# Two more blocks in an SBUF arena, router weights loaded later, and the sync queue in written order behind the router

## The chip, the cores and the metric

The kernel runs on one core of a Trainium2 chip. The metric is the device time of one execution in microseconds. The kernel before took 1211.18 us (median of three runs, 1209.35 to 1215.85).

## The reference

One layer of a streaming encoder for 256 tokens of width 1024: two token mixers with one input projection, a merge by sigmoid gates, a layer norm, then a mixture of 32 experts of which each token takes four, and a second layer norm. Cut to what matters:

```python
mod = silu(c) @ w_ada + b_ada                       # shift1, scale1, gate1, shift2, scale2, gate2
h = x * (1 + scale1) + shift1
q_a, k_a, v_a, c_q, c_kv, k_rope, g_a, g_b = split(h @ w_in)
y_a = chunked_relpos_attention(q_a, k_a, v_a, rel_bias)
y_b = mla_attention(c_q, c_kv, k_rope, positions, ...)
merged = sigmoid(g_a) * (y_a @ w_branch_a) + sigmoid(g_b) * (y_b @ w_branch_b)
x = layer_norm(ALPHA * x + gate1 * (merged @ w_out), ln1_g, ln1_b)
h = x * (1 + scale2) + shift2
logits = h @ w_router + b_router                    # top 4 of 32, softmax over the four
g = min(xb @ w_gate[e] + b_gate[e], 7); up = clip(xb @ w_up[e] + b_up[e], -7, 7)
y = ((up + 1) * g * sigmoid(1.702 * g)) @ w_down[e] + b_down[e]
x = layer_norm(ALPHA * x + gate2 * weighted_sum(y), ln2_g, ln2_b)
```

Each expert has three float32 matrices of 1024 by 1024, so the experts alone are 403 MB of weights.

## The kernel before

**The arena.** Large buffers are blocks of 128 partitions by 2048 float32 values, 1 MB each. There are NB = 20 of them. `al()` hands out the block that has been free longest, `fr()` gives one back. The list PLACES says in which order 18 of them lie in SBUF; the other two (STAY) lie apart. Whatever is loaded, split or computed up to the router lives in such blocks. A load into a block waits until the last reader of its former content is done.

**The stages.** Modulation and the first projection come first (`modulate`, `project`), then attention, gates and the second part of the modulation (`attend`, `z_pair`, `ada2`), whose instructions a scheduler puts in order when the program is built. Then come the merge and the router, written out by hand inside a manual schedule of TensorE, ScalarE, VectorE, GpSimd and SyncE (SP). There `load_branch` and `load_wo` fetch projection weights, `mod_rows` writes the modulation rows to DRAM (tensor `rowd`) and reads them back as columns and as the broadcast rows gate1 and gate2, `o_part` is the output projection, and `route`, `count` and `place` choose the experts. `mod_cols` multiplies the router weights `wr` by the modulation.

**The first two experts** (30 and 31, group "s") are fixed: `load_fixed` fetches their 24 blocks (gate, up and down, four quarters each for two experts) while merge and router still run. In the page and in the matmul names, `sg`, `su` and `sd` are their gate, up and down products. Each product has steps k = 0 to 7, and after each odd step two blocks are given back.

**The other 30 experts** are sorted by how many tokens chose them and run in 13 groups, e0 to e12, of two or three experts. `sort_b` writes the sorted list to `order_i`. For each group SP reads the experts' numbers from it into registers (`nc.sync.value_load`, L1442), and uses them in the addresses of the weight loads (`load_group`, L1126). These loads go to pairs of neighbouring blocks, tensors `wt0` to `wt8`, 2 MB each. Pair d lies over the places 2d and 2d + 1 of PLACES, and `al2()` takes the pair that has been free longest. So each product of a group of two experts takes four pairs.

In the second stretch, from the fixed experts to the last group, only TensorE is under the manual schedule (`pe_cm`, L1383). SP's instructions there stand where the scheduler put them. All DMAs but two are issued by SP, which runs its queue in order: a load that waits holds back all that stands behind it. ScalarE issues the two others, ln1_g and ln1_b at L1080 and L1081, 512 KB each.

Of the kernel before, what the change touches and what calls it, by code (L numbers as in the profile page):

```python
# [8 lines left out]
F32 = mybir.dt.float32  # L9
# [8 lines left out]
P = 128  # L18
D = 1024
S = 256  # L20
E = 32
# [8 lines left out]
SCALE_A = 64.0 ** -0.5  # L30
SCALE_B = 96.0 ** -0.5
CAP = 64
NB = 20
BLK = 2048

STAY = (NB - 2, NB - 1)
PLACES = [10, 8, 1, 2, 0, 12, 13, 16, 11, 7, 4, 14, 5, 15, 6, 9, 17, 3]
FREQS = [
    1.0, 0.5623413324356079, 0.3162277638912201, 0.17782793939113617,
    0.10000000149011612, 0.05623413249850273, 0.03162277489900589, 0.017782794311642647,  # L40
# [28 lines left out]
def bcast_rows(ap, n=P):  # L69
    return bass.AP(tensor=ap.tensor, offset=ap.offset, ap=[[0, n]] + [list(a) for a in ap.ap])  # L70
# [3 lines left out]
def tile_layer(  # L74
# [30 lines left out]
    nc = tc.nc  # L105
    V, A, G, T, SP = nc.vector, nc.scalar, nc.gpsimd, nc.tensor, nc.sync

    const = ctx.enter_context(tc.tile_pool(name="const", bufs=1, side="left"))
# [10 lines left out]
    def ps_t(tag, bufs, name):  # L119
# [7 lines left out]
    first = {i: (aw if i in STAY else ar).tile([P, BLK], F32, tag=f"blk{i}", bufs=1, name=f"blk{i}_0")  # L127
             for i in STAY + tuple(PLACES)}
    freed = {i: i - NB for i in range(NB)}
    clock = [0]  # L130
# [15 lines left out]
    def fr(*blocks):  # L146
        for i in blocks:
            clock[0] += 1
            assert i not in freed
            freed[i] = clock[0]  # L150
# [4 lines left out]
    def ps_b(name):  # L155
        return ps_t("B", nb[0], name)
# [33 lines left out]
    def load_start(b):  # L190
        av, wv = [], []
        for i in range(2):
            v, r = al()
            v = v.rearrange("p (k m) -> p k m", k=8)
            SP.dma_start(v, wada_v[:, :, i * D + b * 256:i * D + (b + 1) * 256])
            av.append((v, r))
        for kk in range(2):
            v, r = al()
            SP.dma_start(v[:, 0:NZ], win_v[:, 2 * b + kk, 1024:1024 + NZ])
            wv.append((v, r))  # L200
        return av, wv
# [13 lines left out]
    LS = [load_start(0), load_start(1)]  # L215
    rows2 = p2.tile([16, P], F32, name="rows2")
    c2 = const.tile([P, 6, 2, 8], F32, name="c2")
    wr = const.tile([P, 8, E], F32, name="wr")
    br_b = const.tile([P, E], F32, name="br_b")
    pos_i = p2.tile([P, 2], I32, name="pos_i")  # L220
    with nc.allow_non_contiguous_dma("one position per partition"):
# [53 lines left out]
    for j in range(4):  # L275
        ps = ps_b(f"xT{j}")
        for kk in range(2):
            for t in range(2):
                k = 2 * j + kk
# [18 lines left out]
    def modulate(b):  # L298
        av, wv = LS[b]
        pm = ps_b(f"gemv{b}")  # L300
        for s in range(2):
            for i in range(2):
                for j in range(4):
                    k = 2 * j + i
                    T.matmul(pm[32 * j:32 * j + 32, s * 256:(s + 1) * 256], crep[:, k, :], av[s][0][:, k, :],
                             start=(i == 0), stop=(i == 1))
        fr(av[0][1], av[1][1])
        md = p2.tile([P, 512], F32, tag="md", bufs=2, name=f"md{b}")
        V.tensor_copy(md, pm)
        pt = ps_b(f"gemvT{b}")  # L310
        for i in range(4):
            T.matmul(pt[:, i:i + 1], md[:, i * P:(i + 1) * P], pick, start=True, stop=True)
        V.tensor_add(sh1v[:, :, 2 * b:2 * b + 2], pt[:, 0:4].rearrange("p (s k) -> p s k", s=2),
                     badv[:, :, 2 * b:2 * b + 2])
        for kk in range(2):
            k = 2 * b + kk
            h32 = p2.tile([P, S], F32, tag="h32", bufs=3, name=f"h32_{k}")
            V.tensor_scalar(h32, xT[:, k, :], sh1[:, 8 + k:9 + k], sh1[:, k:k + 1], op0=ALU.mult, op1=ALU.add)
            split(h32, hTh[:, k, :], hTl[:, k, :], "V")
# [22 lines left out]
    def load_biases():  # L342
        v, r = al()
        for i, b in enumerate((b_gate, b_up, b_down)):
            SP.dma_start(v[32 * i:32 * i + 32, 0:D], b[0])
        return v, r
# [14 lines left out]
    for b in range(4):  # L361
        if b + 2 < 4:
            LS.append(load_start(b + 2))
        if b == 0:
            bias_raw = load_biases()
        if b == 1:
            SP.dma_start(rows2[0:8, :], ln1_g.rearrange("o (k p) -> (o k) p", p=P))
            SP.dma_start(rows2[8:16, :], ln1_b.rearrange("o (k p) -> (o k) p", p=P))
            SP.dma_start(wr, w_router[0].rearrange("(k p) e -> p k e", p=P))
            with nc.allow_non_contiguous_dma("eight values per partition"):  # L370
                SP.dma_start(c2[:, 0, 1, :], ln1_g[0].rearrange("(p k) -> p k", k=8))
                SP.dma_start(c2[:, 1, 1, :], ln1_b[0].rearrange("(p k) -> p k", k=8))
            SP.dma_start(br_b, bcast_rows(b_router[0]))
        if b + 1 < 4:
            modulate(b + 1)
        project(b)
        if b == 1:
            split_biases(*bias_raw)
# [351 lines left out]
    p3 = p3_cm.__enter__()  # L730
# [12 lines left out]
    def mod_rows():  # L743
        for st in range(2):
            ps = ps_b(f"mod2_{st}")
            for j in range(4):
                T.matmul(ps[32 * j:32 * j + 32, :], ones[:, 0:32], acc_b[st][0][:, j * 512:(j + 1) * 512],
                         start=True, stop=True)
            V.tensor_add(rows32[:, st, :], ps, badd[:, st, :])
        fr(acc_b[0][1], acc_b[1][1])  # L750
        fr(ms_r)
        rowd = dram.tile([4 * D], F32, name="rowd")
        for st in range(2):
            SP.dma_start(rowd[st * 2 * D:(st + 1) * 2 * D].rearrange("(j n) -> j n", j=4), rows32[0:P:32, st, :])
        with nc.allow_non_contiguous_dma("a column from a row"):
            SP.dma_start(c2[:, 2:4, 1, :], rowd[D:3 * D].rearrange("(i p k) -> p i k", i=2, k=8))
            for i in range(2):
                SP.dma_start(c2[:, 2 + i, 0, :], rowd[(1 + i) * D:(2 + i) * D].rearrange("(k p) -> p k", p=P))
        SP.dma_start(gate1, bcast_rows(rowd[0:D]))
        SP.dma_start(gate2, bcast_rows(rowd[3 * D:4 * D]))  # L760

    wrs = p3.tile([P, 8, 2, E], F32, name="wrs")
    wrsum = p3.tile([P, 2 * E], F32, name="wrsum")
    gsum = p3.tile([P, E], F32, name="gsum")
# [21 lines left out]
    engines = {e.engine for e in (T, A, V, G, SP)}  # L786
# [12 lines left out]
    def load_fixed(n):  # L799

        for _ in range(n):
            kind, kq, j = fixed_todo.pop(0)
            v, r = al(stay=kind == 0)
            v = v.rearrange("p (k n) -> p k n", k=2)
            SP.dma_start(v, rows_of(weights[kind], E - 2 + j)[:, 2 * kq:2 * kq + 2, :])
            fixed[kind][0][j].append(v)
            fixed[kind][1][j].append(r)
# [2 lines left out]
    load_branch(2)  # L810
    load_branch(3)
    load_fixed(3)
    mod_rows()
    split_branch(1)
    split_branch(2)
# [283 lines left out]
    def open_pairs():  # L1099

        assert all(i in freed for i in PLACES)
        for d in range(len(PLACES) // 2):
            pairs[d] = max(freed[i] for i in PLACES[2 * d:2 * d + 2])
        ar_cm.__exit__(None, None, None)
# [275 lines left out]
        if i < len(GROUPS):  # L1380
            tokens[i] = gather(f"e{i}", group_slots(i))

    pe_cm = tc.manual_schedule(engines={T.engine})  # L1383
    pe_cm.__enter__()
    expert_group("s", segments((64, 64)), gather("s", None), lambda t, j: wtok[:, t, E - 2 + j:E - 1 + j], fixed_w,
                w_bias(sel0.rearrange("p a n -> p (a n)")), {("g", 0): sort_a, ("g", 3): sort_b, ("g", 7): sort_c},
# [134 lines left out]
```

## Time and profile before

| what | value |
|---|---|
| median of three runs | 1211.18 us |
| the profiled execution | 1212.23 us |
| its span, first to last instruction | 1210.5 us |
| mean granted TensorE clock | 0.935 |
| TensorE busy | 1049.7 us, 87% |
| VectorE busy | 372.6 us, 31% |
| HBM read | 462.24 MB, 383 GB/s over the span |

Busy shares are means over stages that have different limits. The page's second part cuts the span into 40 slices of 30.3 us: the DMA engines move 426 GB/s in nearly every slice from the eleventh on, and between 197 and 416 GB/s in the third to tenth. So the first quarter of the time and the rest are read separately.

### The profile page before, as it was taken

Reading aid. Unit: us, or ns where it says so; the run is one execution under the profiler, and the core shown is the slowest. Engines: PE = TensorE matmul, PEld = TensorE weight load, DVE = VectorE, ACT = ScalarE, POOL = GpSimd, SP = SyncE. Lnnn points to the kernel's source line nnn. Section 1 sums busy time; section 2 is a strip of 40 time slices with the busy share of each in tenths; the row PEclk is TensorE's granted clock in tenths of the full one; section 3 lists DMA queues with packets and bytes.
Section 4 is the critical chain, followed back from the end, with each engine's and each line's share of the span. In section 5 each row is a group of like instructions: output and inputs, shape, how many; then the busy total and the mean of one; then the engine's idle time right before and its main releaser. Section 6 shows DMA issues by size and latency. Waiting matters only on the chain.

```text
span 1210.5 us, 18672 instructions
## 1 busy us (share of the span) xinstructions
PE 1049.7 (87%) x7991; PEld 475.7 (39%) x7991; DVE 372.6 (31%) x751; ACT 176.3 (15%) x363; POOL 96.8 (8%) x120
## 2 busy tenths in 40 slices
PE   6889899889999999997768868868779898989895
PEld 4668788754343323332212312312324242424231
DVE  4777995864112112211101101101102030303024
ACT  3346554321000000000000000000000000101001
POOL 2121555300000000000000000000000000000000
PEclk8889999999999999998888888889889999999998
DMA  9968657997999999999999999999999999999992
GB/s 338 328 214 296 244 197 246 365 416 290 426 425 428 425 426 426 427 426 427 426 429 425 428 426 426 428 427 426 427 427 426 426 424 428 426 427 426 426 400 79
DMA packets 68204, 464.55 MB, mean 384 GB/s; under 512 B 8698, under 2 KB 33319, under 8 KB 39959
## 3 DMA queue, kind: packets, MB, share of 16 engines
q1 hardware_dynamic: 67830, 462.28, 93.2%
q8 instruction: 64, 1.05, 0.3%
q10 hardware_dynamic: 288, 1.05, 0.3%
q14 instruction: 22, 0.17, 0.0%
HBM read 462.24 MB, written 1.06 MB: 383 GB/s over the span
## 4 chain that ended last, share of the span: by engine, by line
DMA 48%; PE 40%; DVE 5%; SPq 2%; ACT 2%; issue 1%; POOL 1%; DVEq 0%; ACTq 0%; POOLq 0%
DMA wt<-in_w_gate_dram 21%; DMA wt<-in_w_up_dram 20%; DMA wt<-in_w_down_dram 5%; PE e12d L1172 1%; PE e11d L1172 1%; PE e0d L1172 1%; PE sd L1172 1%; PE e1u L1172 1%; PE e0u L1172 1%; PE e1g L1172 1%; PE e0g L1172 1%; PE e2u L1172 1%; PE su L1172 1%; DMA blk<-in_b_down_dram 1%; DVE blk L649 1%
## 5 line engine op out<-in xcount | busy, mean ns | idle before, releaser
L1215 ACT ACTIVATE blk<-blk 128x512 f32<-128x512 f32 x28 | 17.2, 630 | 532.4 <-DVE blk L1213 532.3
L160 POOL TENSOR_TENSOR blk<-blk,blk 128x512 fp32r<-128x512 f32 (+2 forms) x44 | 82.6, 1896 | 146.5 <-ACT blk L159 89.5
L1446 POOL COPY sel<-sel 96x64 bf16<-96x64 bf16 (+2 forms) x30 | 5.9, 231 | 832.4 <-PE e6d L1263 88.7
L159 ACT CAST blk<-blk 128x512 fp32r<-128x512 f32 (+2 forms) x76 | 53.7, 767 | 38.9 <-DVE blk L862 12.2
L160 DVE TENSOR_TENSOR blk<-blk,blk 128x512 fp32r<-128x512 f32 (+2 forms) x32 | 39.6, 1244 | 20.7 <-ACT blk L159 16.3
L649 DVE SCALAR_TENSOR_TENSOR blk<-blk,csil,blk 128x1024 f32<-128x1024 f32 x28 | 40.4, 1476 | 1.0 <-DMA blk<-in_w_ada_dram 0.9
L287 PE MATMUL g<-blk,blk 128*128 128x256 f32 x128 | 37.3, 294 | 1.8 <-POOL blk L160 1.4
L285 PE MATMUL g<-blk,blk 128*128 128x256 f32 x128 | 37.5, 293 | 0.2 <-ACT blk L159 0.2
L286 PE MATMUL g<-blk,blk 128*128 128x256 f32 x128 | 37.2, 291 | 0.0
L1172 PE MATMUL e6g<-wt,xgb 128*32 128x512 f32 x128 | 20.6, 734 | 9.0 <-DMA wt<-in_w_gate_dram 9.0
L1172 PE MATMUL e7g<-wt,xgb 128*32 128x512 f32 x128 | 21.4, 745 | 7.9 <-DMA wt<-in_w_gate_dram 7.7
L1172 PE MATMUL e4g<-wt,xgb 128*32 128x512 f32 x128 | 20.7, 748 | 8.5 <-DMA wt<-in_w_gate_dram 8.5
L1172 PE MATMUL e5g<-wt,blk 128*32 128x512 f32 x128 | 19.5, 694 | 7.7 <-DMA wt<-in_w_gate_dram 7.7
L287 PEld LDWEIGHTS g<-blk,blk 128*128 128x128 f32 x128 | 24.9, 196 | 3.1 <-POOL blk L160 2.2
L286 PEld LDWEIGHTS g<-blk,blk 128*128 128x128 f32 x128 | 25.1, 196 | 1.2 <-issue 1.2
L285 PEld LDWEIGHTS g<-blk,blk 128*128 128x128 f32 x128 | 25.2, 197 | 0.8 <-ACT blk L159 0.5
L1172 PE MATMUL e6u<-wt,xgb 128*32 128x512 f32 x128 | 19.7, 691 | 6.5 <-DMA wt<-in_w_up_dram 6.5
L1172 PE MATMUL e5u<-wt,blk 128*32 128x512 f32 x128 | 19.3, 699 | 6.9 <-DMA wt<-in_w_up_dram 6.9
L1172 PE MATMUL e4u<-wt,xgb 128*32 128x512 f32 x128 | 19.5, 696 | 6.5 <-DMA wt<-in_w_up_dram 6.5
L1172 PE MATMUL e7u<-wt,xgb 128*32 128x512 f32 x128 | 19.7, 694 | 6.3 <-DMA wt<-in_w_up_dram 6.3
L1172 PE MATMUL e5d<-wt,blk 128*32 128x512 f32 x128 | 18.2, 661 | 6.9 <-DMA wt<-in_w_down_dram 6.5
L1172 PE MATMUL e4d<-wt,xgb 128*32 128x512 f32 x128 | 17.8, 655 | 5.6 <-DMA wt<-in_w_down_dram 5.4
(738 smaller groups left out, 1844.0 us busy)
## 6 DMA issues: line engine op xcount, KB each, us to landing
wt<-in_w_gate_dram SPq DMA_DIRECT2D x60, 2048.0 KB, 30.4
wt<-in_w_up_dram SPq DMA_DIRECT2D x60, 2048.0 KB, 30.3
wt<-in_w_down_dram SPq DMA_DIRECT2D x58, 2048.0 KB, 32.9
blk<-in_w_ada_dram SPq DMA_DIRECT2D x24, 1024.0 KB, 8.8
blk<-in_w_in_dram SPq DMA_DIRECT2D x12, 1024.0 KB, 5.3
blk<-in_w_gate_dram SPq DMA_DIRECT2D x8, 1024.0 KB, 8.0
blk<-in_w_up_dram SPq DMA_DIRECT2D x8, 1024.0 KB, 13.7
blk<-in_w_down_dram SPq DMA_DIRECT2D x8, 1024.0 KB, 10.0
```

Source lines behind the costliest of these rows:

```text
L159: A.copy(hi, src)
L160: (V if eng == "V" else G).tensor_sub(lo, src, hi.bitcast(F32))
L285: T.matmul(o, sh, mh, start=first, stop=False)
L286: T.matmul(o, sh, ml, start=False, stop=False)
L287: T.matmul(o, sl, mh, start=False, stop=last)
L649: eng.scalar_tensor_tensor(acc_v[:, sl], v[:, q * D:(q + 1) * D], csil[:, k:k + 1], acc_v[:, sl], op0=ALU.mult, op1=ALU.add)
L1172: T.matmul(pss[hf][c0:c0 + m, :], stat[:, k, c0:c0 + m], ch[par][k // 2][:, k % 2, hf * 512:(hf + 1) * 512], start=(k == 0), stop=(fine an ...
L1215: A.activation(s, g[:, sl], AF.Sigmoid, scale=SW_ALPHA)
L1446: G.tensor_copy(sel[:, lo:lo + n], sel96[:, r:r + 1].to_broadcast([96, n]))
```

## The change

The arena grows from 20 to 22 blocks, and PLACES gets a new order with 20 entries, so there are ten pairs instead of nine. The SBUF reserved for descriptors of software transfers is set to 1024 bytes per partition. The router weights `wr` move from a constant tile that was loaded during the second projection step to a tile of the merge stage, loaded behind the first three fixed blocks. The manual schedule that begins behind the router now has SP in it as well as TensorE.

```diff
-NB = 20
+NB = 22
-PLACES = [10, 8, 1, 2, 0, 12, 13, 16, 11, 7, 4, 14, 5, 15, 6, 9, 17, 3]
+PLACES = [16, 11, 9, 19, 12, 0, 3, 5, 13, 14, 17, 7, 10, 8, 18, 1, 2, 4, 6, 15]
-    wr = const.tile([P, 8, E], F32, name="wr")
-            SP.dma_start(wr, w_router[0].rearrange("(k p) e -> p k e", p=P))
+    wr = p3.tile([P, 8, E], F32, name="wr")
     load_branch(2)
     load_branch(3)
     load_fixed(3)
+    SP.dma_start(wr, w_router[0].rearrange("(k p) e -> p k e", p=P))
     mod_rows()
-    pe_cm = tc.manual_schedule(engines={T.engine})
+    pe_cm = tc.manual_schedule(engines={T.engine, SP.engine})
-    nc = _bacc.Bacc("TRN2", target_bir_lowering=False, num_devices=1)
+    nc = _bacc.Bacc("TRN2", target_bir_lowering=False, num_devices=1, dynamic_dma_scratch_size=1024)
```

SP's queue between the fixed experts and the first group, before. `blk` is a block, `wt` a pair, `TENSOR_LOAD order_i` the read of one expert's number; seven of these reads stand ahead of the block in the middle and 23 behind it:

```order
L805 DMA blk9_300_2916<-in_w_down_dram 128x2048
L805 DMA blk17_301_2918<-in_w_down_dram 128x2048
L1442 TENSOR_LOAD order_i_2642
L1442 ISA x2
...
L805 DMA blk3_302_2920<-in_w_down_dram 128x2048
L1442 TENSOR_LOAD order_i_2642
...
L1126 ISA
L1126 DMA wt0_0_2996<-in_w_gate_dram 128x4096
L1126 ISA
L1126 DMA wt1_0_2997<-in_w_gate_dram 128x4096
```

The same place now:

```order
L804 DMA blk6_301_2918<-in_w_down_dram 128x2048
L804 DMA blk15_302_2920<-in_w_down_dram 128x2048
L1442 TENSOR_LOAD order_i_2642
L1442 ISA x2
L1442 TENSOR_LOAD order_i_2642
L1442 ISA x2
L1126 ISA
L1126 DMA wt0_0_2996<-in_w_gate_dram 128x4096
...
L1126 DMA wt1_330_3253<-in_w_down_dram 128x4096
L1442 TENSOR_LOAD order_i_2642
L1442 ISA x2
```

Two reads stand ahead of the first pair instead of 30. The other 28 stand in twos and threes ahead of the first load of each later group.

SP's queue at the start of the merge, before, with what the instructions wait for (`DMAHW` is an earlier DMA of the same lane, of which there are eight, taken in turn):

```order
L805 DMA blk18_207_2007<-in_w_gate_dram 128x2048 [waits DVE_49,DMAHW2_49,PE_49,Pool_49]
L805 DMA blk6_208_2009<-in_w_gate_dram 128x2048 [waits Activation_49]
L805 DMA blk9_209_2011<-in_w_gate_dram 128x2048 [waits DMAHW4_49]
L754 DMA rowd_2025<-blk11_181_1837 4x512 [waits DMAHW5_49,DVE_49]
L754 DMA rowd_2025<-blk11_181_1837 4x512 [waits DMAHW6_49,DVE_49]
```

And now:

```order
L804 DMA blk20_207_2006<-in_w_gate_dram 128x2048 [waits DMAHW1_49]
L804 DMA blk21_208_2008<-in_w_gate_dram 128x2048 [waits DMAHW2_49]
L804 DMA blk6_209_2010<-in_w_gate_dram 128x2048 [waits DMAHW3_49]
L812 DMA wr_1990<-in_w_router_dram 128x8x32 [waits DMAHW4_49]
L752 DMA rowd_2025<-blk4_181_1835 4x512 [waits DMAHW5_49,DVE_49]
L752 DMA rowd_2025<-blk4_181_1835 4x512 [waits DMAHW6_49,DVE_49]
```

The three gate blocks wait for no engine any more, since the blocks that they get have been free for longer, and the router weights stand between them and the modulation rows.

## Rows read from the trace of the kernel before

**Rows 1.** The page, part 4: shares of the chain that ended last.
```profile
DMA 48%; PE 40%; DVE 5%; SPq 2%; ACT 2%; issue 1%; POOL 1%; DVEq 0%; ACTq 0%; POOLq 0%
DMA wt<-in_w_gate_dram 21%; DMA wt<-in_w_up_dram 20%; DMA wt<-in_w_down_dram 5%; PE e12d L1172 1%; PE e11d L1172 1%; PE e0d L1172 1%; PE sd L1172 1%; PE e1u L1172 1%; PE e0u L1172 1%; PE e1g L1172 1%; PE e0g L1172 1%; PE e2u L1172 1%; PE su L1172 1%; DMA blk<-in_b_down_dram 1%; DVE blk L649 1%
```

**Rows 2.** Windows: busy time of each engine, clock, DMA share and rate.
```profile
core 0: us, PE busy (x) PEld busy (x) DVE busy (x) ACT busy (x) POOL busy (x), PEclk, DMA share, GB/s
235.00:272.00 37.00, 33.08 (x213) 23.79 (x217) 25.88 (x95) 8.77 (x19) 1.23 (x1) 0.91 1.01 419
272.00:296.00 24.00, 24.00 (x231) 9.22 (x225) 11.58 (x19) 1.26 (x2) 0.86 (x4) 1.00 0.66 251
285.00:290.00 5.00, 5.00 (x52) 1.70 (x48) 5.00 (x4) 0.00 (x0) 0.00 (x0) 1.00 0.00 0
290.00:295.00 5.00, 5.00 (x49) 1.56 (x42) 0.14 (x1) 0.00 (x0) 0.00 (x0) 1.00 0.82 298
400.00:1150.00 750.00, 638.43 (x4873) 217.28 (x4876) 119.14 (x245) 43.17 (x86) 4.61 (x24) 0.92 1.01 426
```

**Rows 3.** Timeline of SP's DMA issues around the gap: start, us, count.
```profile
266.63 9.62 SPq L805 DMA_DIRECT2D blk<-in_w_down_dram  x4
...
289.92 2.11 SPq L1126 DMA_DIRECT2D wt<-in_w_gate_dram  x4
```

**Rows 4.** Timeline of VectorE: the sorted list is written.
```profile
271.41 0.18 DVE L1293 CAST order_i<-order 1x32 int32<-1x32 f32 x1 [0.40 <-PE order L1292]
```

**Rows 5.** Chain in order of time: start us, us, what.
```profile
271.92 7.00 PE sg L1172 x64
...
281.10 13.77 PE su L1172 x128
...
314.58 13.87 PE e0g L1172 x128
...
366.72 13.87 PE e1g L1172 x128
...
399.16 33.42 DMA wt<-in_w_gate_dram
```

**Rows 6.** DMA issues by line: count, KB each, median us from issue to landing.
```profile
wt<-in_w_gate_dram SPq DMA_DIRECT2D x60, 2048.0 KB, 30.4
...
blk<-in_ln_g_dram ACTq DMA_DIRECT2D x1, 512.0 KB
blk<-in_ln_b_dram ACTq DMA_DIRECT2D x1, 512.0 KB
```

**Rows 7.** Timeline of SP's DMA issues at the start of the merge.
```profile
189.24 0.96 SPq L672 DMA_DIRECT2D blk<-in_w_branch_b_dram  x1
195.47 1.29 SPq L805 DMA_DIRECT2D blk<-in_w_gate_dram  x3
197.18 1.33 SPq L754 DMA_DIRECT2D rowd<-blk  x2
205.42 0.39 SPq L756 DMA_DIRECT2D c<-rowd  x1
...
208.19 1.23 SPq L825 DMA_DIRECT2D blk<-in_w_out_dram  x2
```

**Rows 8.** SP's waits: for whom, us in total, times, longest.
```profile
SPq L805 <- PE g L287: 5.1, 1, 5.1
```

**Rows 9.** Timeline: ScalarE begins to split the first output weights.
```profile
216.61 2.00 ACT L159 CAST blk<-blk 128x1024 fp32r<-128x1024 f32 x2 [2.00 <-DMA blk<-in_w_out_dram]
```

**Rows 10.** The router weights' instructions: duration ns min/median/max, first and last start us.
```profile
L369 SPq DMA_DIRECT2D wr<-in_w_router_dram x1: 1427/1427/1427, 35.8 to 35.8; - x1
```

**Rows 11.** Windows of the attention stage, columns as in Rows 2.
```profile
62.00:196.00 134.00, 124.08 (x893) 104.96 (x895) 109.97 (x210) 72.45 (x183) 54.17 (x37) 0.96 0.67 235
140.00:150.00 10.00, 7.06 (x53) 5.98 (x52) 9.68 (x14) 8.58 (x22) 5.72 (x4) 0.99 0.98 350
```

**Rows 12.** The page, part 3: DMA queues, packets, MB, share of 16 engines.
```profile
q1 hardware_dynamic: 67830, 462.28, 93.2%
q8 instruction: 64, 1.05, 0.3%
q10 hardware_dynamic: 288, 1.05, 0.3%
q14 instruction: 22, 0.17, 0.0%
```

## The prediction

> **What bounds the kernel now.** I read the chain of waits first. Nearly half of it is weight transfers of the expert groups, and the products of the first groups follow [rows 1]. In order of time the chain lies on TensorE up to 399 us, and from there on each group waits for a transfer [rows 5]. The windows say the same from the other side: from 400 to 1150 us the DMA engines are busy without a break at 426 GB/s, while TensorE has 112 us to spare [rows 2]. So the end is set by when the last weight byte lands, and that by the last time the queue ran dry. It is in the windows too: 235 to 272 us is dense at 419 GB/s, 272 to 296 us has a mean of 251, and between 285 and 290 us nothing moves at all [rows 2]. Bytes not moved there are moved at the end.
>
> Why it ran dry is seen in SP's issues. The last fixed block is issued by 276.25 us, the first pair at 289.92 us [rows 3]. In between SP reads the experts' numbers. The list is there at 271.59 us [rows 4], 30 reads stand ahead of the first pair and 23 of them behind the last block, so one read takes (289.92 - 276.25) / 23 = 0.594 us. At 289.92 us four pairs go out within 2.11 us [rows 3], so the first pairs had been free already.
>
> **The reads that move (the main term).** Now two reads stand ahead of the first pair, ready at 271.59 + 2 x 0.594 = 272.8 us. What counts next is when a pair is free. I followed the rule of the blocks through the merge by hand. The first pair lies over the two blocks of the third gate quarter, the second over the fourth, then come two of up for each further pair. Of sg the last four steps take 7.00 us from 271.92 us [rows 5], 1.75 us a step, so step 5 is done at 275.4 us and step 7 at 278.9 us. Before, the first pair lay over the fourth quarter, free at 278.9 us. The up blocks come free in twos every 13.77 / 4 = 3.44 us from 281.10 us on [rows 5]: 284.5, 288.0, 291.4, 294.9 us. A pair of 2.097 MB takes 4.92 us at 426 GB/s, so once the stream runs, pairs come free faster than it fills them.
>
> The gain has two bounds. From below: the fixed blocks land when they did and pairs fill the hole behind them. Missing there are (426 - 251) x 24 / 426 = 9.9 us [rows 2]. From above: all fixed blocks have landed by 275.4 us, because two more blocks let them start sooner. Then the stream starts 289.9 - 275.4 = 14.5 us sooner, but ScalarE's two loads of together 1.05 MB [rows 6], which fell in the hole, now take 2.5 us of the stream: 12.0 us. I take 11: the fixed blocks do start sooner, but not all waits in the merge are for blocks.
>
> The Trainium skill (DMA: Bandwidth & Descriptors, Specifications) puts the limit of HBM per core at about 358 GB/s. By that the missing 4.2 MB would be worth 11.7 us; the trace disagrees, with 426 GB/s over 750 us, and the measurement decides.
>
> **The other 28 reads** now stand in twos and threes ahead of groups, 1.2 or 1.8 us each time. Behind each wait SP's weight loads. What covers them is the queue: a pair lands 30.4 us (median) after its issue [rows 6], some six transfers of 4.92 us. I cost them at nothing; with no cover they cost 28 x 0.594 = 16.6 us.
>
> **Does TensorE become the bound?** From e0g to e1g it takes 366.72 - 314.58 = 52.1 us for a group [rows 5]; the group's 12 pairs take 59.0 us of DMA. It starts e0g at 314.58 us whatever the stream does, since sg, su and sd stand back to back before it. By then a stream begun at 278 us (ScalarE's loads out of the way) has filled 7.4 of ten pairs. The eleventh pair is wanted at 278 + 49 = 327 us and is the first one again, given back at half of e0g, 321.5 us. So the stream does not stall, and each group it falls back 7 us against TensorE. With nine pairs it would be wanted at 322, just in time. The tenth pair is thus worth little by itself.
>
> **The merge.** Before, the three gate blocks waited 5.1 us for products of the gates [rows 8] and went out at 195.47 us; the branch weights ahead were out at 190.2 us [rows 7]. Now they wait for no engine, so 3.1 MB enter the queue some 5 us sooner. The modulation rows go out at 197.18 us as before but have less ahead of them: they are awaited until 205.42 us [rows 7], and I expect some 2 us less. Then the output weights (208.19 us) are issued sooner, and ScalarE waits for these until 216.61 us [rows 9]. Against it, the router weights now stand ahead of the rows: 128 KB, 0.3 us by bytes, up to 1.4 us by the issue that SP needed for them [rows 10]; I take 0.5. It is between 0 and 3 us gained, and I take 1.5, because TensorE's own products leave room for no more.
>
> On the router weights the skill's same page and section say that a transfer reaches line rate only from 512 bytes a run; these have runs of 128 bytes. By a fourfold price they would cost 1.2 us, within the 1.4 us above, so the sum stays; no row shows their landing.
>
> **Start and attention.** Here the scheduler orders all engines, and with other blocks it orders them differently. TensorE is idle 9.9 of the 134 us from 62 to 196 us, 2.9 of them from 140 to 150 us [rows 11], so 10 us is the most that can be gained. For a loss the nearest row is the same idle time, doubled. Two more blocks let loads start sooner; another order may lose as much. I take 0, and -5 to +6 us as likely bounds. The early load of the router weights goes, 0.3 us by bytes.
>
> **Reserve.** I cost it at nothing: the queues listed are hardware queues and instruction fetches [rows 12], none is software's.
>
> **Sum.** 11 + 1.5 + 0 = 12.5 us. The profiled execution took 1212.23 us (span 1210.5 and 1.7 around it), so 1199.7; the median lies 1.05 us lower, so I forecast 1198.7 us. The terms' own bounds give 1212.2 - (12 + 3 + 5) = 1192 and 1212.2 - (9.9 + 0 - 6) = 1208.
>
> **The rivals.**
> - *The reads are not hidden.* If SP reaches a group's first load with an empty queue, all 28 reads show, 16.6 us, and each of the 12 starts also pays what the stream needs to start: from 290 to 295 us it moved 298 of 426 GB/s [rows 2], 1.5 us lost. Together 34.6 us, so 1199.7 + 34.6 - 1.05 = 1233 us, slower than before. It begins where less than 1.8 us of transfers are in flight at a group's start, and decides where over a third of it shows. Against it are the 30.4 us to landing [rows 6]. 6%.
> - *Attention is ordered worse.* A loss of some 9 us there, about all of TensorE's idle time once more, gives 1208 us. For it: no block rule says that this stage gains. Against: TensorE is 93% busy there [rows 11] with the same work. 13%.
> - *Attention is ordered better.* Half the idle time and the start's waits go, some 8 us: 1191 us. For it: loads there wait for blocks. 14%.
> - *The hole moves.* If the earlier fixed blocks only bring the queue to its end sooner, it is empty until the first pair at 275.4 us and again for lack of free pairs, and half the main term is lost: 1204 us. Against it are the 3.44 us in which pairs come free. 8%.
> - *The smaller reserve throttles the queue.* Then every 1% of rate costs 8.9 us over the 890 us of stream; 1% gives 1208 us. Nothing in the queue list speaks for it [rows 12]. 2%.
>
> The forecast itself, 1195 to 1203 us, has the remaining 57%.
>
> **How the numbers follow.** About 0.5%, 6 us, is what a measurement of this kernel can tell from no change. Faster by that (below 1205.1) are the forecast, the better attention, the moved hole and some of the worse attention: 83%. Within it falls the rest of the worse attention and most of the reserve's case: 11%. Slower are the unhidden reads: 6%. The range reaches from the better attention with the full main term (1189) to the worse attention (1208).
>
> **What would show it.** In the profile after, SP issues the first pair at about 275 us instead of 289.92, counted from a sg at the same time. The windows from 235 to 300 us show 420 GB/s or more throughout. The three gate blocks go out at about 190 us. From 320 us to the last group DMA stays at 426 GB/s, with 1.2 to 1.8 us between a group's last and first issue at most. The distance from sg to the end is shorter by 11 us, and sg's last steps begin within some 6 us of 271.92 us. The prediction is wrong if the stream has holes at the groups' starts, if those steps start more than 6 us later, or if the stream's rate is below 420.

## The result, and the profile after

The changed kernel takes 1222.85 us (median of 5 runs, 1220.16 to 1225.89), against 1211.18 us for the kernel before (1209.35 to 1215.85). The ratio is 1.0093, 95% interval 1.0075 to 1.0111: 0.9% slower, where I forecast 1198.7 us. The profiled execution of after is the longest of its five (1225.89 us, span 1223.8).

Page of the profile after, part 4, answering [rows 1]: DMA's share falls from 48% to 44% and VectorE's rises from 5% to 8%. New among the lines is the softmax (`p L612`), beside the modulation products (`blk L647`, which is L649 in before).

```profile
DMA 44%; PE 42%; DVE 8%; ACT 2%; issue 2%; SPq 1%; POOL 0%; DVEq 0%; ACTq 0%; POOLq 0%
DMA wt<-in_w_gate_dram 30%; DMA wt<-in_w_up_dram 12%; DVE blk L647 1%; DVE p L612 1%; DVE blk L160 1%; PE e12d L1172 1%; PE e1d L1172 1%; PE e0d L1172 1%; PE sd L1172 1%; PE e1u L1172 1%; PE e12u L1172 1%; PE e2g L1172 1%; PE e0u L1172 1%; PE e1g L1172 1%; PE e0g L1172 1%
```

What the change was made for happened. Windows of after, answering [rows 2 and 11]; columns as there:

```profile
62.00:196.00 134.00, 116.17 (x794) 97.45 (x794) 103.35 (x205) 62.73 (x168) 41.08 (x28) 0.94 0.64 215
272.00:296.00 24.00, 20.70 (x162) 13.35 (x165) 15.47 (x63) 7.48 (x15) 0.00 (x0) 0.93 1.01 418
400.00:1150.00 750.00, 645.32 (x4994) 221.79 (x4990) 125.33 (x257) 44.39 (x88) 4.61 (x24) 0.92 1.01 426
```

SP's issues in after, answering [rows 3 and 7] (start, us, count; the last row is the first pair):

```profile
209.72 0.37 SPq L670 DMA_DIRECT2D blk<-in_w_branch_a_dram  x1
...
211.78 1.49 SPq L804 DMA_DIRECT2D blk<-in_w_gate_dram  x3
213.32 0.43 SPq L812 DMA_DIRECT2D wr<-in_w_router_dram  x1
219.38 3.92 SPq L752 DMA_DIRECT2D rowd<-blk  x2
227.82 0.38 SPq L754 DMA_DIRECT2D c<-rowd  x1
...
270.88 23.13 SPq L804 DMA_DIRECT2D blk<-in_w_down_dram  x8
298.74 12.83 SPq L1126 DMA_DIRECT2D wt<-in_w_gate_dram  x4
```

The first pair goes out while the fixed blocks still land, and from 272 to 296 us the stream moves 418 GB/s, where before it moved 251 [rows 2]. But everything is 22 us late: the rows of the modulation go out at 219.38 us instead of 197.18 [rows 7].

**An account by the stream.** From 400 us on the stream moves 426 GB/s in both kernels, so what it failed to move earlier is added at the end. (The stream is all that the DMA engines move, nearly all of it weights.) In a window I call the length times (1 - rate / 426) its *shortfall*. Windows of before:

```profile
0.00:100.00 100.00, 79.24 (x516) 60.60 (x517) 62.38 (x147) 38.72 (x76) 24.45 (x48) 0.90 0.83 276
100.00:170.00 70.00, 66.47 (x496) 58.91 (x495) 65.16 (x117) 37.72 (x107) 30.80 (x20) 0.98 0.74 264
170.00:230.00 60.00, 57.26 (x427) 51.45 (x426) 41.24 (x43) 30.02 (x46) 27.18 (x15) 1.00 0.83 287
0.00:270.00 270.00, 237.98 (x1649) 196.12 (x1649) 198.43 (x399) 117.23 (x248) 88.39 (x88) 0.94 0.83 293
270.00:330.00 60.00, 58.61 (x550) 22.70 (x551) 18.67 (x37) 4.51 (x9) 0.86 (x4) 1.00 0.87 355
```

The same windows of after:

```profile
0.00:100.00 100.00, 73.92 (x457) 55.47 (x458) 53.02 (x128) 33.27 (x66) 20.98 (x46) 0.85 0.85 286
100.00:170.00 70.00, 61.37 (x465) 56.05 (x464) 63.73 (x108) 35.55 (x93) 27.86 (x19) 0.98 0.72 248
170.00:230.00 60.00, 51.56 (x376) 44.55 (x375) 37.47 (x54) 28.92 (x60) 25.39 (x15) 0.94 0.47 161
0.00:270.00 270.00, 222.75 (x1495) 186.59 (x1496) 184.09 (x341) 108.23 (x231) 85.18 (x88) 0.92 0.76 263
270.00:330.00 60.00, 56.23 (x490) 29.52 (x492) 30.24 (x90) 12.17 (x25) 0.86 (x4) 0.97 1.01 422
```

To 270 us the shortfall is 270 x (1 - 293/426) = 84.3 us before and 103.3 after: 19.0 lost. From 270 to 330 us it is 10.0 before and 0.6 after: 9.4 gained. The spans are 1210.5 and 1223.8, so 13.3 - 19.0 + 9.4 = 3.7 us are left for the end (first experiment). The loss has one place. Up to 100 us after is ahead by 1.0 MB, and from 100 to 170 us it loses 1.1 MB; from 170 to 230 us it moves 161 GB/s instead of 287, 7.6 MB or 17.7 us less. So the start's own delay (the first qpe product at 79.6 instead of 72.5 us) does not by itself put the stream behind.

What happens there, in after's chain of waits (start us, us, what):

```profile
189.69 3.50 DMA blk<-in_w_branch_a_dram
193.30 1.04 ACT blk L159
194.62 1.77 ACT p L604 x8
196.62 3.05 DVE p L612 x4
206.94 0.58 PE y L625 x2
...
211.40 2.55 POOL blk L160 x2
217.60 1.90 PE mod L745 x16
```

Three windows of after, with TensorE's busy time in the first column behind the length, and SP's longest wait between 170 and 230 us (in total, times, longest):

```profile
180.00:190.00 10.00, 9.33 (x73) 8.11 (x72) 7.14 (x18) 5.29 (x14) 0.27 (x1) 1.00 0.06 19
190.00:200.00 10.00, 3.92 (x25) 2.73 (x26) 7.23 (x15) 7.78 (x19) 6.08 (x4) 0.88 0.33 105
200.00:210.00 10.00, 9.89 (x59) 8.71 (x58) 2.15 (x3) 7.06 (x11) 1.28 (x3) 0.78 0.01 2
```

```profile
SPq L670 <- PE g L286: 30.7, 2, 19.1
```

The last head pair's exponentials (`p L604`) begin at 194.6 us; before it was 171.3. What ScalarE does for gate projections 6 and 7 is queued behind them (`issue_after` in the kernel). So TensorE runs dry, and the branch weights (L670), the next thing to load, wait for blocks that gate projections hold, up to 19.1 us: 2 GB/s from 200 to 210 us. TensorE's queue shows why the softmax is late. A head pair has eight score products; these are the ones from 140 us on, first in before (the last pair's), then in after (the last three pairs', the last eight from 189.9 us on):

```profile
L583 PE MATMUL s<-blk x8: 269/324/480, 142.8 to 143.4; 64*128 64x256 f32 x4, 64*128 64x128 f32 x4
```

```profile
L581 PE MATMUL s<-blk x24: 269/374/480, 152.2 to 191.4; 64*128 64x256 f32 x12, 64*128 64x128 f32 x12
```

In before the last scores stand ahead of gate projection 2, at 143 us; in after they stand behind gate projection 5, at 190 us.

### The profile page after: what moved, and what is told of

It reads as the page before. It is cut to its first block, busy times and chain, and to the rows that moved or that the text cites. A ratio compares the mean times of both kernels' runs of the same rounds, so it can differ in the third digit from the quotient of the medians.

```text
span 1223.8 us, 18664 instructions
## 1 busy us (share of the span) xinstructions
PE 1049.6 (86%) x7991; PEld 480.0 (39%) x7991; DVE 372.4 (30%) x751; ACT 175.4 (14%) x363; POOL 93.6 (8%) x120
## 4 chain that ended last, share of the span: by engine, by line
DMA 44%; PE 42%; DVE 8%; ACT 2%; issue 2%; SPq 1%; POOL 0%; DVEq 0%; ACTq 0%; POOLq 0%
DMA wt<-in_w_gate_dram 30%; DMA wt<-in_w_up_dram 12%; DVE blk L647 1%; DVE p L612 1%; DVE blk L160 1%; PE e12d L1172 1%; PE e1d L1172 1%; PE e0d L1172 1%; PE sd L1172 1%; PE e1u L1172 1%; PE e12u L1172 1%; PE e2g L1172 1%; PE e0u L1172 1%; PE e1g L1172 1%; PE e0g L1172 1%
## 5 line engine op out<-in xcount | busy, mean ns | idle before, releaser
L160 POOL TENSOR_TENSOR blk<-blk,blk 128x512 fp32r<-128x512 f32 (+2 forms) x44 | 79.2, 1817 | 169.7 <-ACT blk L159 116.5
L647 DVE SCALAR_TENSOR_TENSOR blk<-blk,csil,blk 128x1024 f32<-128x1024 f32 x28 | 39.3, 1435 | 3.2 <-DMA blk<-in_w_ada_dram 3.2
L1172 PE MATMUL e6d<-wt,xgb 128*32 128x512 f32 x128 | 17.9, 658 | 5.5 <-DMA wt<-in_w_down_dram 5.2
## 6 DMA issues: line engine op xcount, KB each, us to landing
wt<-in_w_gate_dram SPq DMA_DIRECT2D x60, 2048.0 KB, 37.4
wt<-in_w_up_dram SPq DMA_DIRECT2D x60, 2048.0 KB, 37.4
```

The costliest lines, as they stand in the source:

```text
L160: (V if eng == "V" else G).tensor_sub(lo, src, hi.bitcast(F32))
L647: eng.scalar_tensor_tensor(acc_v[:, sl], v[:, q * D:(q + 1) * D], csil[:, k:k + 1], acc_v[:, sl], op0=ALU.mult, op1=ALU.add)
L1172: T.matmul(pss[hf][c0:c0 + m, :], stat[:, k, c0:c0 + m], ch[par][k // 2][:, k % 2, hf * 512:(hf + 1) * 512], start=(k == 0), stop=(fine an ...
```

## The experiments

All times are medians of 4 to 12 runs in us; ratios are to the kernel before on the same chip. Shortfall is to 270 us, and from 270 to 330 us; it and the span are of the one profiled execution.

| run | time | ratio, 95% | shortfall | span |
|---|---|---|---|---|
| before | 1211.18 | | 84.3, 10.0 | 1210.5 |
| after | 1222.85 | 1.0093 (1.0075 to 1.0111) | 103.3, 0.6 | 1223.8 |
| e1 SP's order alone | 1205.81 | 0.9959 (0.9943 to 0.9975) | 84.3, 0.3 | 1203.7 |
| e2 wr and reserve alone | 1214.69 | 1.0026 (1.0013 to 1.0039) | 87.5, 9.3 | 1215.1 |
| e3 after without SP's order | 1234.49 | 1.0192 (1.0166 to 1.0218) | 102.0, 13.0 | 1233.2 |
| e4 two blocks only from the merge | 1207.55 | 0.9966 (0.9950 to 0.9982) | 83.7, 0.7 | 1203.6 |
| e5 products behind the maxima | 1228.98 | 1.0131 (1.0113 to 1.0149) | 102.7, 6.2 | 1227.3 |
| e6 two blocks from attention on | 1221.25 | 1.0074 (1.0057 to 1.0090) | 100.8, 0.4 | 1221.4 |
| e7 one block from the start | 1205.96 | 0.9953 (0.9936 to 0.9969) | 83.0, 0.1 | 1203.4 |
| e8 new order, 20 blocks | 1208.97 | 0.9960 (0.9943 to 0.9976) | 87.5, 0.7 | 1207.7 |
| e9 last scores early | 1215.97 | 1.0027 (1.0007 to 1.0048) | 94.4, 0.3 | 1214.7 |
| e10 e9 + e5 | 1216.17 | 1.0028 (1.0012 to 1.0044) | 94.4, 0.4 | 1214.3 |
| e11 gate 6 not held | 1216.15 | 1.0028 (1.0008 to 1.0047) | 95.7, 0.6 | 1214.1 |
| e12 e9 + e5 + e11 | 1213.14 | 1.0005 (0.9988 to 1.0023) | 91.3, 0.1 | 1211.1 |
| e13 e12 + second softmax | 1213.44 | 1.0017 (0.9999 to 1.0035) | 91.3, 0.3 | 1209.8 |
| e14 second softmax alone | 1218.26 | 1.0050 (1.0030 to 1.0070) | 98.2, 0.4 | 1218.6 |
| e15 e12, after's blocks | 1219.33 | 1.0058 (1.0040 to 1.0076) | 97.6, 0.7 | 1216.5 |
| e16 e9 + e11 + half of e5 | 1216.00 | 1.0023 (1.0003 to 1.0044) | 95.7, 0.4 | 1215.4 |

Span less both shortfalls is 1117.8 to 1120.3 us in every run but before, which has 1210.5 - 94.3 = 1116.2. So the two windows account for a difference between two changed kernels to within 2.5 us, and against before there are 1.6 to 4.1 us more. Before's own median lay between 1211.2 and 1212.6 us from chip to chip, so differences between medians of two chips are good to about 1 us.

**e1: SP's written order alone**

```diff
-    pe_cm = tc.manual_schedule(engines={T.engine})
+    pe_cm = tc.manual_schedule(engines={T.engine, SP.engine})
```

> Kernel before with one edit: SP's instructions in written order behind the router; 20 blocks, wr and reserve as before. Theory A (the loss of the change lies wholly ahead of the merge and comes from the two more blocks; the gain behind sg comes from SP's order alone): start and attention as before, sg's last half starts at 271.9 us within 2, first pair issued 3 to 8 us behind that, and 8 to 11 us gained, so 1200 to 1203 us. Rival B (the gain behind sg needs the two blocks too, since with nine pairs the queue runs dry again): at most half of it, 1206 to 1211 us.

The gap closes wholly: the first pair goes out at 277.43 us, and the shortfall falls by 9.7 us. The time falls by 5.9 us only, between A's range and B's, and not for B's reason, since with nine pairs the queue does not run dry. Some 3 us are lost again behind these windows. The chain's last wait for a transfer, first in before, then in e1, then in e2 (below), whose gap is open:

```profile
1131.98 32.65 DMA wt<-in_w_up_dram
1164.67 7.06 PE e12u L1172 x60
```

```profile
1102.16 34.00 DMA wt<-in_w_gate_dram
1136.20 8.40 PE e12g L1172 x60
...
1149.25 13.87 PE e12u L1172 x128
```

```profile
1115.75 31.60 DMA wt<-in_w_gate_dram
1147.39 8.76 PE e12g L1172 x60
```

Before, the last group still waits for its up weights, until 45.8 us before the end. In e1 these are there in time, and from its gate weights on the chain waits for no transfer: 67.5 us to the end. It is tempting to say that the closed gap makes the last group TensorE's and so loses 3 us here and 3.7 in after. But e2 ends in the same way, 67.7 us from its gate weights to the end, and it too has 2.1 us more than before, with 9.3 us of gap. So the loss at the end is measured, and its cause stays open.

**e2: the router weights and the reserve; e3: after without SP's order; e4: the blocks late.** e2 moves the load of `wr` and shrinks the reserve, nothing else; e3 takes e1's line back from after; e4 is after with (main lines):

```diff
-    freed = {i: i - NB for i in range(NB)}
+    freed = {i: i - NB for i in range(NB) if i not in LATE}
...
     load_fixed(3)
     SP.dma_start(wr, w_router[0].rearrange("(k p) e -> p k e", p=P))
+    freed.update({i: i - NB for i in LATE})
     mod_rows()
```

LATE are the two more blocks. The list of places was fitted anew to the order in which blocks come free, here and in e6, e7, e8, e10, e12 and e13.

> Kernel before with the router weights loaded at the merge and the smaller reserve; 20 blocks, SP as before. Theory A: neither matters, 1210 to 1213 us, the merge's first matmul at 195.3 us within 2. Rival C (the late load of the router weights, the smaller reserve or the few instructions that the scheduler moves for them cost the 22 us): 1225 to 1235 us.

> Kernel after without SP's written order; 22 blocks, wr at the merge, small reserve. Theory A: the front's loss without the gain behind sg: merge's first matmul at 217.6 us within 2, and 1231 to 1235 us. Rival D (SP's written order itself reaches into the front, by a part of the 22 us): 1222 us or less, merge's first matmul clearly before 217.

> Kernel after, but the two more blocks are handed in only at the merge, behind the loads of the branch weights and of three gate quarters: start and attention run with 20 blocks, all else is as in after. Theory A: start and attention as before (merge's first matmul at 195.3 us within 2), the gain behind sg in full, 9 to 12 us: 1199 to 1203 us, so faster than both kernels. Rival C: still slower than before, over 1220 us. Rival B': the two blocks in the merge add something to SP's order alone, 2 us or more below the run with SP's order alone.

e2 costs 3.0 us, not 22: C falls as the main cause, but A's "neither matters" was not right either. In e2 SP's issue of the second row of the modulation takes 4.66 us, against 0.56 before. That long issue does not by itself put the stream behind: e4 has the same load and nearly the same issue, and its shortfall is 83.7. e4's two rows of the modulation (duration in ns min/median/max), then the windows to 190 us of e2 and of e4:

```profile
L753 SPq DMA_DIRECT2D rowd<-blk x2: 668/2579/4490, 197.3 to 201.9; - x2
```

```profile
0.00:190.00 190.00, 160.77 (x1144) 133.70 (x1144) 144.01 (x280) 90.62 (x209) 64.91 (x75) 0.95 0.76 260
0.00:190.00 190.00, 162.57 (x1155) 134.47 (x1156) 145.30 (x281) 91.90 (x211) 66.54 (x76) 0.95 0.77 264
```

e2 is behind by 190 us already, ahead of the moved load: 260 GB/s against 264 in e4 and in before, 1.8 us. So part of its loss comes before that load, where a few instructions stand elsewhere; the rest was not separated. e3 has after's front (merge's first matmul at 215.8 us) and a worse gap than before, 13.0 us; from 300 to 310 us it moved 11 GB/s. There the two blocks bring the fixed weights to their end sooner, and nothing follows: the rival of the moved hole, which SP's order hides in after (1234.5 - 1222.9 = 11.6 us). e4 puts the front back (195.1 us) and keeps the closed gap. It is 15.3 us faster than after and 7.1 faster than e2, whose front is much the same (196.9 us); its median is above A's range, its mechanism is A's. B' falls: e4 is not below e1 (1207.55 against 1205.81 us), so the two blocks add nothing in the merge either. So the loss comes from the two blocks, in the stages ahead of the merge.

**e6, e7, e8: how many blocks, and where.** e6 hands the two blocks in behind the start's projections; e7 has one of them from the start and the other at the merge; e8 has 20 until the merge but hands both in before its first load, which alone makes the scheduler order start and attention anew.

> Kernel after, but the two more blocks are handed in behind the start's projections: start with 20 blocks, attention with 22, and attention's order nearly that of after (no product of the modulation rows behind the last head pair's maxima). Theory A (two separate losses, 7 us in the start and 15 in attention): qpe at 72 to 75 us as before, merge's first matmul at 207 to 212 us, 1212 to 1218 us. Rival F (the start's delay is the cause, attention only carries it on): merge's first matmul at 195 to 199 us, 1199 to 1205 us. Rival F' (the start costs nothing in the end, attention's order all of it): merge's first matmul at 215 us or later, 1219 us or more.

> Kernel after with one more block in start and attention (21) and the other handed in at the merge. Rival G (the loss goes with the number of blocks, each brings half of it): merge's first matmul at 206 us within 3, 1209 to 1214 us. Theory A (it goes by what order the scheduler finds, not by the number): two products of the modulation rows stand behind the last maxima, against six in before and none in after, so about 5 us lost there, and the start like that of after, 7 us: merge's first matmul at 207 us within 4. If it comes out below 200 or above 214 us the number of blocks says nothing at all.

> Kernel after, start and attention with 20 blocks, and the two more handed in at the very beginning of the merge instead of behind its first loads. That alone makes the scheduler order start and attention anew (about as many TensorE instructions stand elsewhere as between before and after), with the same number of blocks; six products of the modulation rows stand behind the last maxima, as in before. Theory A: no loss where these products stay behind: merge's first matmul at 193 to 199 us, 1199 to 1206 us. Rival H (before's order was the good draw, and any new order loses): merge's first matmul at 205 us or later, over 1212 us.

e6 has 100.8 - 84.3 = 16.5 of after's 19.0 us: F' holds, and the start accounts for at most 2.5 us. e7 loses nothing; its merge begins at 202.1 us, in none of the ranges, but its stream is not behind, 83.0. So the loss does not go by the number of blocks (G falls; my estimate for A fell too). e8, whose order differs from before's nearly as much as after's does, has 87.5, as e2 has (A; the time is 3 us above its range). e7's order differs as much, and it shows that a new order need not cost anything, so H falls: after's is a bad one. In both the last scores stand early, as in before; e7, then e8:

```profile
L582 PE MATMUL s<-blk x16: 269/324/480, 145.9 to 150.3; 64*128 64x256 f32 x8, 64*128 64x128 f32 x8
L582 PE MATMUL s<-blk x16: 269/374/480, 149.1 to 152.0; 64*128 64x256 f32 x8, 64*128 64x128 f32 x8
```

The place of the last scores goes with the loss in the other runs too. Where the last of them starts by 152 us (before, e1, e2, e4, e7, e8), the shortfall to 270 us is 83.0 to 87.5; where it starts at 187.9 us or later (after, e3, e5, e6, e11, e14), it is 95.7 to 103.3.

**e5, e9, e10, e11, e12: what is bad in it.** e5 queues the last eight modulation products behind the last maxima on VectorE; e9 traces the last pair's attention earlier and queues gate projections 4 and 5 behind its scores; e11 does not hold gate projection 6 behind the last exponentials. e10 is e9 and e5, e12 all three. The edits, cut to the main lines:

```diff
 e5
+            with tc.issue_after(last_neg.ins):
+                ada2(6)
+                ada2(7)
 e9
+        if i == 2:
+            last_exp = attend(0, 3)
...
+        elif i == 2:
+            with tc.issue_after(last_s[0].ins):
+                gate_pair(2 * i)
 e11
-            with tc.issue_after(last_exp.ins):
-                gate_pair(6)
+            gate_pair(6)
```

> Kernel after (22 blocks), but the last eight VectorE products of the modulation rows (two calls of ada2) are put in VectorE's queue behind the maxima of the last head pair; the scheduler orders the rest anew around it. As in before, six of them then stand behind those maxima, where after has none. Theory A (in attention the loss is the order: VectorE does these products first, so the last softmax is late, and the two gate projections that are queued behind it start late): 6 x 1.23 = 7.4 us come back, the last exponentials end at 187 to 191 us instead of 196.3, the merge's first matmul stands at 209 to 212 us, and the time is 1213 to 1218 us. Rival E (the softmax is late because its loads and the start are late): all within 3 us of after, 1220 to 1225 us.

> Kernel after, but the score products of the last head pair are traced and queued on TensorE ahead of the gate projections 4 and 5, instead of behind them. Up to the scores of the pair before (172 us) every engine's order is word for word that of after. Theory B (with 22 blocks the scheduler lets gate projections run ahead of the last score products; the last softmax is late for that, and two gate projections, and with them blocks and loads, are held behind it): scores of the last pair at 174 us instead of 190, last exponentials end at 187 to 192 us instead of 196.3 (VectorE still has the modulation products ahead of them), merge's first matmul at 209 to 214 us, 1215 to 1219 us. Rival I (the score products' place is a symptom; blocks or loads set the end of attention): merge's first matmul within 2 us of 217.5, 1220 to 1225 us.

> As the run with the scores early, and in addition the last eight products of the modulation rows queued on VectorE behind the last head pair's maxima (alone these brought nothing, since VectorE then waited from 180 to 190 us for the scores). Theory B: the two together take away both things that stand ahead of the last softmax: last exponentials end at 178 to 184 us, merge's first matmul at 201 to 207 us, 1206 to 1213 us, about before's time or better with 22 blocks in the front. Rival I: 1218 us or more.

> Kernel after, but the gate projection 6 is no longer held behind the last exponentials (its sigmoid is then taken with those of the other pairs). Order word for word that of after up to the last pair's scores at 190 us. Theory B: its 48 products fill TensorE's idle time between 191 and 207 us: TensorE busy 8 us or more of 190 to 200 us instead of 3.9, merge's first matmul 4 to 7 us earlier (211 to 214 us), 1215 to 1219 us. Rival I: TensorE has the products but the branch weights still wait for blocks: 1220 to 1225 us.

> Kernel after with the three edits together: scores early, modulation products behind, gate 6 not held. Theory B: merge's first matmul at 197 to 204 us, 1203 to 1210 us, as fast as the best so far (SP's order alone, 1205.8 us). Rival I: over 1215 us.

e5's theory fell. The last exponentials still end at 196 us, because VectorE now waits for scores: 0.4 us busy from 180 to 190. (Of its 6 us on top of after, 5.6 are a gap from 270 us on, probably because its places were not fitted to the order in which its blocks come free.) That led to e9, and e9 and e11 came out as theory B said, with 6.9 and 6.7 us back; by the ratios to before it is 8.0 and 7.9. Scores of e9, then the window of e11 in which TensorE was busy for 3.92 us in after:

```profile
L583 PE MATMUL s<-blk x24: 269/374/480, 149.5 to 172.3; 64*128 64x256 f32 x12, 64*128 64x128 f32 x12
```

```profile
190.00:200.00 10.00, 8.67 (x65) 7.25 (x63) 3.40 (x13) 8.10 (x16) 2.71 (x2) 1.00 0.41 124
```

Merge's first matmul stands at 209.2 and 211.1 us, both in B's ranges. With this the two links, scores behind gates and gates behind softmax, are shown. But they do not add up: e10 and e16 give no more than e9, which neither theory had for e10. e12 gives 9.7 us, 12.0 of 19.0 by the shortfall; its time is above B's range.

**e13 to e16: the other part**

> As the run with the three edits, and in addition the second set of modulation products (ada2 of 1) queued on VectorE behind the second head pair's maxima. In after these products stand ahead of that softmax and wait for a load from 102.8 to 106.0 us, and VectorE, which is busy all the time from 110 us on, stands idle some 6 us more between 90 and 110 us than in before. Theory K (that is the other half of attention's loss): the second pair's exponentials end at 105 to 112 us instead of 127.6, merge's first matmul at 200 to 206 us, 1203 to 1209 us. Rival J (the rest is the start's 7 us, or loads that wait for blocks): 1211 to 1216 us, as with three edits.

> Kernel after with only that edit: the second set of modulation products queued behind the second head pair's maxima; the last pair's scores still stand behind the gate projections. Theory K: VectorE gets 5 to 6 us back and the whole chain behind it comes earlier by that: merge's first matmul at 210 to 214 us, 1214 to 1219 us. Rival J: the late scores set the end of attention whatever VectorE does before: 1220 to 1225 us.

> The three edits once more (last scores early, the last eight modulation products behind the last maxima, gate 6 not held), but with blocks handed out in exactly the order of after. In the earlier run of the three edits the last modulation loads asked for their blocks later than in after, and nothing was moved from 170 to 180 us. Theory L (that was a by-product of the edit and hid the rest of the gain): DMA moves over 100 GB/s from 170 to 180 us, merge's first matmul at 200 to 206 us, 1204 to 1209 us. Rival M (the rest of the loss does not hang on the place of the last scores, products and gate): 1211 to 1216 us.

> Kernel after with the last scores early, gate 6 not held, and only the last four modulation products behind the last maxima; blocks handed out in the order of after. Theory L: each of the first two gave 7 us alone; together they fill the same idle time of TensorE in part, so 10 to 13 us: merge's first matmul at 203 to 208 us, 1208 to 1213 us. Rival M: no more than either alone, 1214 us or more.

e14 alone brings 4.6 us back, as K said (VectorE no longer waits for a load at 106 us with a softmax queued behind), but nothing on top of e12. e15 makes the same three edits as e12, and hands the blocks out as after does; transfers do go on from 170 to 180 us (108 GB/s, 3 in e12), yet it is 6.2 us slower, outside both ranges. L falls. The order in which blocks are handed out is thus worth as much here as one of the edits. In after's order three edits bring 5 to 7 us each, and together they bring less than their sum; that they fill the same idle time of TensorE is my reading. The last 7 us of shortfall (91.3 in e12 against 83.7 in e4) stay open. One rival for them is untested: e9 and all runs with its edit bring the last scores to 172 to 176 us only (shortfall 91.3 to 97.6), and no run with 22 blocks in attention has them at 143 us, where before has them.

No edit of after's attention beats before. The runs without its loss and with SP's order, e1, e4, e7 and e8, beat both kernels, by ratios of 0.9953 to 0.9966 to before.

## Why the prediction was wrong

**The reads that move (11, bounds 9.9 to 12.0): right in mechanism.** The gap in the stream closes, 9.4 us in after and 9.7 in e1. The first pair was to follow the first of sg's last four steps: these begin at 295.11 us, and 298.74 is 3.6 behind. What the sum lacks is the end: some 3 us are lost there, for a cause that stays open, so alone the edit brings 5.9 us. From sg's last steps to the end after has 928.7 us against 938.6, 9.9 less, which looks like the term; but by its sg at 286 us after had moved 77.8 MB (272 GB/s), before 76.2 by 262.8 (290 GB/s), worth 3.7 us.

**The other 28 reads at nothing: right.** From 400 to 1150 us it is 426 GB/s [rows 2], and a pair lands 37.4 us after its issue, longer than before's 30.4 [rows 6].

**The tenth pair is worth little: right.** e1 with nine pairs has no gap either.

**The merge (-1.5, 0 to 3): too hopeful.** From its first matmul to sg it takes 286.0 - 217.5 = 68.5 us, before 67.5. The three gate blocks do go out right behind the branch weights, at 211.78 us, but the rows are issued for 3.92 us instead of 1.33 [rows 7]. I took 0.5 us for the router weights. The runs do not price them: e2 loses 3.0 us, in part ahead of their load, and e4, which has the same load, is not behind in the stream.

**Start and attention (0, -5 to +6): the step that failed.** I put this term at nothing. It cost 22 us on TensorE and 19.0 in the stream, three times the worse bound, and nearly all of it in attention (e6). I had argued that TensorE's idle time of 9.9 us in the stage [rows 11] measures what an order can win or lose. It measures what can be won; a worse order makes idle time anew. The loss came out of `issue_after`, which stood in the kernel: two gate projections stand behind the last softmax, so whatever delays that softmax delays them in full, and the loads that need their blocks. The working followed the order only at the places that the change was meant for; what would have told, the last scores behind gate 5 instead of ahead of gate 2, can be read from TensorE's order alone: the six kernels that have them by 152 us are the six without the loss. I also took the blocks to help ("two more blocks let loads start sooner"). They do, up to 100 us. That the weights which come sooner are what lets gate projections run ahead of the scores is my reading; no run isolates it.

**The rivals.** The worse attention was among them at 13%, priced at 9 us; twice that came, so its direction was foreseen and its size was not. The moved hole is real but only without SP's order (e3). The reserve shows nothing: 426 GB/s as before.

## What to carry to other kernels

Where a scheduler orders the work, a change of its resources is a change of the order everywhere. Before costing it, compare the orders at every point where a queue is held behind one instruction, and price such a hold by all that stands behind it, not by the stage's idle time. In a kernel bound by one stream, cumulate what the stream failed to move: it gives the place and size of a loss at once, while engine times early in the program (qpe 7 us late) can mean little. And hand out a new resource only in the stage that needs it: e4 does so and loses nothing ahead of the merge, though here the two blocks brought nothing there either.

## What the hardware showed that I had not expected

VectorE's modulation product took 1.2 us alone and 2.1 beside GpSimd. Timeline of after, VectorE, then GpSimd in the same time:

```profile
106.00 4.19 DVE L647 SCALAR_TENSOR_TENSOR blk<-blk,csil,blk 128x1024 f32<-128x1024 f32 x2 [3.18 <-DMA blk<-in_w_ada_dram]
...
116.22 2.47 DVE L647 SCALAR_TENSOR_TENSOR blk<-blk,csil,blk 128x1024 f32<-128x1024 f32 x2
```

```profile
105.59 1.29 POOL L160 TENSOR_TENSOR blk<-blk,blk 128x512 fp32r<-128x512 f32 x1 [8.91 <-ACT blk L159]
107.11 2.00 POOL L160 TENSOR_TENSOR blk<-blk,blk 128x512 fp32r<-128x512 f32 x1 [0.24 <-ACT blk L159]
113.22 2.53 POOL L160 TENSOR_TENSOR blk<-blk,blk 128x512 fp32r<-128x512 f32 x2 [4.11 <-ACT blk L159]
```

The pair at 106.00 us runs beside GpSimd's subtractions, the one at 116.22 us behind the last of them. The Trainium skill (SBUF — State Buffer, Who interferes with whom) says that a VectorE instruction with two inputs in SBUF contends with a GpSimd instruction that reads SBUF; the trace agrees, with 4.19 us for two against 2.47. So an order that only puts such work side by side also makes it longer.

TensorE was busy for 3.92 us only from 190 to 200 us. Its granted clock was 0.88 there and 0.78 from 200 to 210 us, in which it was busy for 9.89 us (windows of after above): part of the time was at the lower of its two levels, 1.2 GHz, just when the held projections came. Products of theirs in after:

```profile
203.89 0.41 PE L284 MATMUL g<-blk,blk 128*128 128x256 f32 x1
204.10 0.41 PE L285 MATMUL g<-blk,blk 128*128 128x256 f32 x1
...
204.51 0.28 PE L284 MATMUL g<-blk,blk 128*128 128x256 f32 x1
204.63 0.28 PE L285 MATMUL g<-blk,blk 128*128 128x256 f32 x1
```

They start 0.21 us apart up to 204.31 us and 0.12 us apart from 204.51 us on. The slow ones reach from 200.33 to 204.31 us, 18 steps, so I estimate that the lower clock cost about 18 x 0.09 = 1.6 us here.
